# A ReLU-and-sum kernel rewritten on its own semaphores, with clamp and sum split between two engines in three 64 KB buffers

## Chip, cores, metric

One core of a Trainium2 chip. The metric is the device time of one execution in microseconds (us), lower is better. A profile's "span" runs from the first to the last instruction of the program. The time is a little longer than the span. Times are medians.

## The reference

```python
x = np.random.randn(32, 512, 1024).astype(np.float32)
return np.sum(np.maximum(x, 0), axis=-1)      # (32, 512), float32
```

That is 16,384 rows of 1024 numbers, 67.1 MB to read and 64 KB to write. Each of the 128 partitions gets 128 rows.

## The kernel before

The rows are loaded in blocks: seven of 16 rows (64 KB per partition, 8 MB in all), then 8, 4, 2 and 1 rows, then the last row in four column pieces. Blocks of 16 and 8 rows share two buffers. Each row is handled whole by one engine: even rows by ScalarE (ReLU with an accumulated sum), odd rows by VectorE (max with 0, summed). A framework decides the waits.

```python
io_pool = ctx.enter_context(tc.tile_pool(name="io", bufs=2))
...
        nc.scalar.activation(out=out_ap, in_=in_ap, func=Relu,
                             accum_out=res[:, m : m + 1])           # line 71
...
        nc.vector.tensor_scalar(out=out_ap, in0=in_ap, scalar1=0.0, scalar2=None,
                                op0=max, op1=add, accum_out=accum_out)  # line 79
...
    for j, cpd in enumerate(chunks):             # 16 x7, then 8, 4, 2, 1
        xt = io_pool.tile([P, cpd, D], fp32, tag="io", ...)
        nc.sync.dma_start(out=xt, in_=...)                          # line 95
        for c in range(cpd):
            m = m0 + c
            if m == NT - 2:
                act_op(...)
                nc.scalar.dma_start(out=out2d[:, 0 : NT - 2], ...)  # first store
            elif (c % 2) == 0: act_op(xt[:, c, :], xt[:, c, :], m)
            else:              dve_op(xt[:, c, :], xt[:, c, :], res[:, m : m + 1])
...
    for i in range(np_ - 1):                     # pieces 244, 252, 260 wide
        dve_op(ptiles[i], ptiles[i], last[:, pieces[-1] + i : ...])
    dve_op(last, last, res[:, m_last : m_last + 1])   # 268 + three partial sums
    nc.sync.dma_start(out=out2d[:, NT - 2 : NT], in_=res[:, NT - 2 : NT])
```

The four pieces are summed one after the other: the first three leave a partial sum each beside the fourth, which adds them up. The last store waits for that.

## Time and profile before

| | before |
|---|---|
| time, median (4 runs) | 163.43 us (163.22 to 163.71) |
| span of the profiled run | 161.5 us |
| VectorE / ScalarE busy | 46% / 43% |
| load queue, share of 16 DMA engines | 96.9% |

From the profile's page: the span, the busy line, the busy tenths of DMA in 40 slices, and the queue list (name, packets, MB, share).

```profile
span 161.5 us, 347 instructions
DVE 74.3 (46%) x134; ACT 69.0 (43%) x129; POOL 0.2 (0%) x4
DMA  8997997996997997997996997997997997999990
q1 hardware_dynamic: 2304, 67.11, 96.9%
q14 instruction: 2, 0.02, 0.0%
```

The DMA line dips to 7 now and then only because a slice of 4.0 us counts the 2.42 us packets that start in it, and some slices hold fewer starts. The table of stretches, cut at the landings of the blocks, is plainer (columns: start and end, length, busy time and count of each engine, granted clock, DMA share, GB/s):

```profile
core 0: us, DVE busy (x) ACT busy (x) POOL busy (x), PEclk, DMA share, GB/s
22.20:41.60 19.40, 9.21 (x16) 8.42 (x16) 0.00 (x0) 1.00 1.00 432
...
119.60:138.90 19.30, 9.21 (x16) 8.42 (x16) 0.00 (x0) 1.00 0.98 423
...
157.50:161.50 4.00, 1.57 (x8) 1.15 (x2) 0.00 (x0) 1.00 0.10 22
```

The load stream is full from the first to the last block, and both engines are idle half of the time. The chain of waits that ended last shows the end of it (start, length, what):

```profile
41.61 9.22 DVE xt L79 x16
...
50.88 29.41 DMA xt<-in_x_dram
...
130.74 26.82 DMA p<-in_x_dram
157.56 0.02 issue
157.58 1.14 DVE p L79 x6
158.72 0.02 issue
158.74 0.43 DVE p L79
```

The wait of those sums, from the list of waits (engine, what waited, for what: us in total, times, longest):

```profile
DVE p L79 <- DMA p<-in_x_dram: 0.4, 1, 0.4
```

Lines with "issue" in a chain are moments in which the profile shows nothing that the engine waited for.

Read the chain from the end: the last piece sum (started 158.74) closes 1.6 us of sums, which wait for the landing of the pieces at 157.56. A load is asked for 9.2 us after the landing of the block whose buffer it takes, then takes 29.4 us, because about 10 us of it is queueing behind the block before. The queue is never empty. The groups by form give the price of one row on each engine (mean ns of one after the comma):

```profile
L79 DVE TENSOR_SCALAR_CACHE_REDUCE xt<-xt 128x1024 f32<-128x1024 f32 x63 | 72.6, 1216 | 84.5 <-DMA xt<-in_x_dram 84.2
L71 ACT ACTIVATE xt<-xt 128x1024 f32<-128x1024 f32 x64 | 66.7, 1043 | 89.0 <-DMA xt<-in_x_dram 89.0
```

### The profile page before, as it was taken

What the parts mean: (1) busy time and instruction counts of PE and PEld (TensorE: products, weight loads), DVE (VectorE), ACT (ScalarE), POOL (GpSimd) and SP (SyncE); (2) the same over time, 40 slices, a digit from 0 to 9 for tenths busy, and PEclk for the clock granted to TensorE, in tenths of its full rate; (3) what the DMA queues carried; (4) which work ended last, traced back from release to release, by engine and by line L of the source; (5) the groups of instructions that cost most, each with busy time, mean ns of one, the idle gap of its engine ahead of it and who ended that gap; (6) DMA issues with size and microseconds to landing.
All of it is one profiled execution on the core that took longest, in us unless ns stands there. A gap on an engine that the chain in (4) does not pass through costs nothing.

```text
span 161.5 us, 347 instructions
## 1 busy us (share of the span) xinstructions
DVE 74.3 (46%) x134; ACT 69.0 (43%) x129; POOL 0.2 (0%) x4
## 2 busy tenths in 40 slices
DVE  0000049700695008940099101991039900598983
ACT  3000049500693008920099001990039700596882
POOL 0000000000000000000000000000000000000000
DMA  8997997996997997997996997997997997999990
GB/s 308 471 503 308 487 487 308 503 503 292 503 503 308 487 503 325 471 519 308 471 519 296 487 503 325 471 503 341 454 503 341 454 503 308 430 438 406 406 359 22
DMA packets 2450, 67.19 MB, mean 416 GB/s; under 512 B 528, under 2 KB 1040, under 8 KB 1168
## 3 DMA queue, kind: packets, MB, share of 16 engines
q1 hardware_dynamic: 2304, 67.11, 96.9%
q10 hardware_dynamic: 144, 0.06, 0.1%
q14 instruction: 2, 0.02, 0.0%
HBM read 67.11 MB, written 0.07 MB: 416 GB/s over the span
## 4 chain that ended last, share of the span: by engine, by line
DMA 79%; DVE 18%; SPq 1%; issue 0%; DVEq 0%
DMA xt<-in_x_dram 62%; DVE xt L79 17%; DMA p<-in_x_dram 17%; SPq L95 1%; DVE p L79 1%; DVEq L79 0%; DVEq L16 0%
## 5 line engine op out<-in xcount | busy, mean ns | idle before, releaser
L79 DVE TENSOR_SCALAR_CACHE_REDUCE xt<-xt 128x1024 f32<-128x1024 f32 x63 | 72.6, 1216 | 84.5 <-DMA xt<-in_x_dram 84.2
L71 ACT ACTIVATE xt<-xt 128x1024 f32<-128x1024 f32 x64 | 66.7, 1043 | 89.0 <-DMA xt<-in_x_dram 89.0
L71 ACT ACTIVATION_READ_ACCUMULATOR xt<-xt 128x1 f32 x64 | 11.9, 187 | 0.0
L79 DVE DVE_READ_ACCUMULATOR xt<-xt 128x1 f32 x63 | 5.2, 83 | 0.0
L79 DVE TENSOR_SCALAR_CACHE_REDUCE p<-p 128x244 f32<-128x244 f32 (+3 forms) x4 | 1.6, 420 | 0.4 <-DMA p<-in_x_dram 0.4
L71 ACT ACT_TABLE_LOAD x1 | 1.3, 1283 | 0.8 <-PEq L143 0.8
L79 DVE DVE_READ_ACCUMULATOR p<-p 128x1 f32 x4 | 0.3, 82 | 0.0
L143 POOL MEMSET const-bfloat16-1.0<- 128x1 bf16 x1 | 0.1, 101 | 0.0
L143 POOL MEMSET const-uint8-127<- 128x1 uint8 x1 | 0.1, 101 | 0.0
L143 POOL MEMSET const-float32-0.0<- 128x1 f32 x1 | 0.1, 98 | 0.2 <-issue 0.2
L143 POOL MEMSET const-float32-1.0<- 128x1 f32 x1 | 0.1, 98 | 0.0
## 6 DMA issues: line engine op xcount, KB each, us to landing
xt<-in_x_dram SPq DMA_DIRECT2D x1, 4096.0 KB, 19.6
xt<-in_x_dram SPq DMA_DIRECT2D x1, 2048.0 KB, 24.2
xt<-in_x_dram SPq DMA_DIRECT2D x1, 1024.0 KB, 26.2
xt<-in_x_dram SPq DMA_DIRECT2D x1, 512.0 KB, 27.0
p<-in_x_dram SPq DMA_DIRECT2D x1, 134.0 KB, 10.0
p<-in_x_dram SPq DMA_DIRECT2D x1, 130.0 KB, 26.5
p<-in_x_dram SPq DMA_DIRECT2D x1, 126.0 KB, 26.7
p<-in_x_dram SPq DMA_DIRECT2D x1, 122.0 KB, 26.8
```

The source lines that it names most:

```text
L71: nc.scalar.activation(out=out_ap, in_=in_ap, func=mybir.ActivationFunctionType.Relu, accum_out=res[:, m : m + 1],)
L79: nc.vector.tensor_scalar(out=out_ap, in0=in_ap, scalar1=0.0, scalar2=None, op0=mybir.AluOpType.max, op1=mybir.AluOpType.add, accum_out=ac ...
L95: nc.sync.dma_start(out=xt, in_=xv[:, m0 * D : (m0 + cpd) * D].rearrange("p (c d) -> p c d", c=cpd),)
L143: nc = _bacc.Bacc("TRN2", target_bir_lowering=False, num_devices=1)
```

## The change

The intent as the diff shows it: far fewer instructions and waits. The framework's scheduling is dropped for hand-placed semaphores; there are three 64 KB buffers instead of two; in the first six blocks ScalarE clamps 16 rows (8 rows in the last three blocks) in one instruction and VectorE sums them in one; the seventh block is done by rows, ten on ScalarE and six on VectorE; the tail and the pieces are as before; both stores are issued by SyncE.

```diff
+ROWS = 16
+NBUF = 3
+STEPS = [16, 16, 16, 8, 8, 8]
+ACT_ROWS = 10
+TAIL = [8, 4, 2, 1]
+PIECES = [244, 252, 260, 268]
...
+    for j, step in enumerate(STEPS):
+        buf = bufs[j % NBUF]
+        loaded = load(buf[:, :, :], xv[:, m : m + ROWS, :], j >= NBUF and freed[j - NBUF])
+        for c in range(0, ROWS, step):
+            clamp(buf[:, c : c + step, :], loaded if c == 0 else None)   # ScalarE, line 77
+            total(buf[:, c : c + step, :], m + c, step)   # VectorE tensor_reduce, line 85
+        freed.append(n_dve)
+        m += ROWS
...
+    for c in range(ROWS):                                 # block 6
+        first = loaded if c in (0, ACT_ROWS) else None
+        if c < ACT_ROWS:
+            act_row(buf[:, c, :], m + c, first)           # line 92
+        else:
+            dve_row(buf[:, c, :], res[:, m + c : m + c + 1], first)   # line 102
...
+    nc.sync.wait_ge(sems.act, n_act - 1)
+    nc.sync.dma_start(out=out2d[:, : NT - 2], in_=res[:, : NT - 2]).wait_op(
+        sems.dve, n_dve, "sem-ge"
+    ).then_inc(sems.stored, 16)
...
+    nc.sync.wait_ge(sems.act, n_act)
+    nc.sync.dma_start(out=out2d[:, NT - 2 :], in_=res[:, NT - 2 :]).wait_op(
+        sems.dve, n_dve, "sem-ge"
+    ).then_inc(sems.stored, 16)
+    nc.sync.wait_ge(sems.stored, 32)
...
-    io_pool = ctx.enter_context(tc.tile_pool(name="io", bufs=2))
-            elif (c % 2) == 0:
-                act_op(xt[:, c, :], xt[:, c, :], m)
-            else:
-                dve_op(xt[:, c, :], xt[:, c, :], res[:, m : m + 1])
```

Blocks are numbered 0 to 6 below.

More of the change, by code (lines that the diff above doesn't have):

```diff
@@ L1 @@
-from contextlib import ExitStack
 import concourse.bass as bass
 import concourse.tile as tile
-from concourse import bass_utils, mybir
-from concourse._compat import with_exitstack
+from concourse import mybir
+F32 = mybir.dt.float32
+RELU = mybir.ActivationFunctionType.Relu
+MAX, ADD = mybir.AluOpType.max, mybir.AluOpType.add
+P = 128
+ROWS = 16
[4 more added lines that the diff above has]
+PIECES = [244, 252, 260, 268]
 EARLY = 1
 def kernel(tc: tile.TileContext, x: bass.AP, out: bass.AP):
-    trace_relu_sum(tc, x, out)
+    nc = tc.nc
+    sems = Semaphores(tc)
@@ L15, with __init__ @@
     tc.close()
     tc.compile()
-    issue_ahead_of_the_barrier(tc, EARLY)
+    nc.cur_bb = nc.bb_map[tc.start_bb_name]
+    body = nc.cur_bb.bb.instructions
+    ends = list(body)
+    body.clear()
+    relu_sum(nc, sems, x, out)
+    body.extend(ends)
+    issue_ahead_of_the_barrier(tc, EARLY)
+class Semaphores:
+    def __init__(self, tc: tile.TileContext):
+        n = len(STEPS) + 1 + len(TAIL) + len(PIECES)
+        self.loads = [tc.alloc_semaphore(f"load{i}") for i in range(n)]
+        self.act = tc.alloc_semaphore("act")
+        self.dve = tc.alloc_semaphore("dve")
+        self.stored = tc.alloc_semaphore("stored")
@@ new lines, in relu_sum, with load, clamp, total @@
+def relu_sum(nc, sems: Semaphores, x: bass.AP, out: bass.AP):
+    x_flat = x.flatten_outer_dims()
+    N, D = x_flat.shape
+    NT = N // P
+    assert N == P * NT == P * (ROWS * (len(STEPS) + 1) + sum(TAIL) + 1)
+    assert sum(TAIL) == ROWS - 1 and sum(PIECES) == D
+    xv = x_flat.rearrange("(p m) d -> p m d", p=P)
+    out2d = out.rearrange("b s -> (b s)").rearrange("(p m) -> p m", p=P)
+    bufs = [nc.alloc_sbuf_tensor(f"io{i}", [P, ROWS, D], F32) for i in range(NBUF)]
+    res = nc.alloc_sbuf_tensor("res", [P, NT], F32)
+    extra = len(PIECES) - 1
+    parts = [
+        nc.alloc_sbuf_tensor(f"piece{i}", [P, w + extra * (i == extra)], F32)
+        for i, w in enumerate(PIECES)
+    ]
+    n_load = n_act = n_dve = 0
+    def load(dst, src, after=None):
+        nonlocal n_load
+        dma = nc.sync.dma_start(out=dst, in_=src)
+        if after:
+            dma.wait_op(sems.dve, after, "sem-ge")
+        dma.then_inc(sems.loads[n_load], 16)
+        n_load += 1
+        return sems.loads[n_load - 1]
+    def clamp(ap, loaded):
+        nonlocal n_act
+        i = nc.scalar.activation(out=ap, in_=ap, func=RELU)
+        if loaded is not None:
+            i.wait_op(loaded, 16, "sem-ge")
+        i.then_inc(sems.act, 1)
+        n_act += 1
+    def total(ap, m, n):
+        nonlocal n_dve
+        nc.vector.tensor_reduce(
+            out=res[:, m : m + n], in_=ap, axis=mybir.AxisListType.X, op=ADD
+        ).wait_op(sems.act, n_act, "sem-ge").then_inc(sems.dve, 1)
+        n_dve += 1
+    def act_row(ap, m, loaded):
+        nonlocal n_act
+        i = nc.scalar.activation(
+            out=ap, in_=ap, func=RELU, accum_out=res[:, m : m + 1]
+        )
+        if loaded is not None:
+            i.wait_op(loaded, 16, "sem-ge")
+        i.then_inc(sems.act, 1)
+        n_act += 1
+    def dve_row(ap, accum_out, loaded):
+        nonlocal n_dve
+        i = nc.vector.tensor_scalar(
+            out=ap,
+            in0=ap,
+            scalar1=0.0,
+            scalar2=None,
+            op0=MAX,
+            op1=ADD,
+            accum_out=accum_out,
+        )
+        if loaded is not None:
+            i.wait_op(loaded, 16, "sem-ge")
+        i.then_inc(sems.dve, 1)
+        n_dve += 1
+    freed = []
+    m = 0
+    for j, step in enumerate(STEPS):
[6 more added lines that the diff above has]
+        m += ROWS
+    j = len(STEPS)
+    buf = bufs[j % NBUF]
+    loaded = load(buf[:, :, :], xv[:, m : m + ROWS, :], freed[j - NBUF])
+    for c in range(ROWS):
[4 more added lines that the diff above has]
+            dve_row(buf[:, c, :], res[:, m + c : m + c + 1], first)
+    m += ROWS
+    buf = bufs[(j + 1) % NBUF]
+    c0 = 0
+    for n in TAIL:
+        loaded = load(
+            buf[:, c0 : c0 + n, :],
+            xv[:, m + c0 : m + c0 + n, :],
+            None if c0 else freed[j + 1 - NBUF],
+        )
+        for c in range(c0, c0 + n):
+            first = loaded if c < c0 + 2 else None
+            if c % 2 == 0:
+                act_row(buf[:, c, :], m + c, first)
+            else:
+                dve_row(buf[:, c, :], res[:, m + c : m + c + 1], first)
+        c0 += n
+    col = 0
+    arrived = []
+    for part, w in zip(parts, PIECES):
+        arrived.append(load(part[:, :w], xv[:, NT - 1, col : col + w]))
+        col += w
+    nc.sync.wait_ge(sems.act, n_act - 1)
+    nc.sync.dma_start(out=out2d[:, : NT - 2], in_=res[:, : NT - 2]).wait_op(
+        sems.dve, n_dve, "sem-ge"
+    ).then_inc(sems.stored, 16)
+    last, w = parts[-1], PIECES[-1]
+    for i in range(extra):
+        dve_row(parts[i][:, :], last[:, w + i : w + i + 1], arrived[i])
+    nc.vector.wait_ge(arrived[-1], 16)
+    before_last = n_dve
+    nc.vector.tensor_scalar(
+        out=last[:, :],
+        in0=last[:, :],
+        scalar1=0.0,
+        scalar2=None,
+        op0=MAX,
+        op1=ADD,
+        accum_out=res[:, NT - 1 : NT],
+    ).wait_op(sems.dve, before_last, "sem-ge").then_inc(sems.dve, 1)
+    n_dve += 1
+    nc.sync.wait_ge(sems.act, n_act)
[3 more added lines that the diff above has]
+    nc.sync.wait_ge(sems.stored, 32)
@@ L36, in issue_ahead_of_the_barrier @@
     opening[at:at] = loads
-@with_exitstack
-def trace_relu_sum(
-    ctx: ExitStack,
-    tc: tile.TileContext,
-    x: bass.AP,
-    out: bass.AP,
-):
-    nc = tc.nc
-    fp32 = mybir.dt.float32
-    P = nc.NUM_PARTITIONS
-    x_flat = x.flatten_outer_dims()
-    N, D = x_flat.shape
-    assert N % P == 0
-    NT = N // P
-    xv = x_flat.rearrange("(p m) d -> p (m d)", p=P)
-    out2d = out.rearrange("b s -> (b s)").rearrange("(p m) -> p m", p=P)
-    big = 16
-    tail = [8, 4, 2, 1]
-    pieces = [244, 252, 260, 268]
-    assert sum(pieces) == D
-    nbig, rem = divmod(NT - sum(tail) - 1, big)
-    assert rem == 0
-    chunks = [big] * nbig + tail
-    io_pool = ctx.enter_context(tc.tile_pool(name="io", bufs=2))
-    res_pool = ctx.enter_context(tc.tile_pool(name="res", bufs=1))
-    res = res_pool.tile([P, NT], fp32)
-    def act_op(in_ap, out_ap, m):
-        nc.scalar.activation(
-            out=out_ap,
-            in_=in_ap,
-            func=mybir.ActivationFunctionType.Relu,
-            accum_out=res[:, m : m + 1],
-        )
-    def dve_op(in_ap, out_ap, accum_out):
-        nc.vector.tensor_scalar(
-            out=out_ap,
-            in0=in_ap,
-            scalar1=0.0,
-            scalar2=None,
-            op0=mybir.AluOpType.max,
-            op1=mybir.AluOpType.add,
-            accum_out=accum_out,
-        )
-    m0 = 0
-    for j, cpd in enumerate(chunks):
-        if cpd >= 8:
-            xt = io_pool.tile([P, cpd, D], fp32, tag="io", name=f"xt{j}")
-        else:
-            xt = io_pool.tile([P, cpd, D], fp32, tag=f"t{cpd}", bufs=1, name=f"xt{j}")
-        nc.sync.dma_start(
-            out=xt,
-            in_=xv[:, m0 * D : (m0 + cpd) * D].rearrange("p (c d) -> p c d", c=cpd),
-        )
-        for c in range(cpd):
-            m = m0 + c
-            if m == NT - 2:
-                act_op(xt[:, c, :], xt[:, c, :], m)
-                nc.scalar.dma_start(out=out2d[:, 0 : NT - 2], in_=res[:, 0 : NT - 2])
-            elif (c % 2) == 0:
-                act_op(xt[:, c, :], xt[:, c, :], m)
-            else:
-                dve_op(xt[:, c, :], xt[:, c, :], res[:, m : m + 1])
-        m0 += cpd
-    m_last = m0
-    assert m_last == NT - 1
-    base = m_last * D
-    np_ = len(pieces)
-    wlast = pieces[-1] + (np_ - 1)
-    ptiles = []
-    col = 0
-    for i, w in enumerate(pieces):
-        shape_w = w if i < np_ - 1 else wlast
-        pt = io_pool.tile([P, shape_w], fp32, tag=f"p{i}", bufs=1, name=f"p{i}")
-        ptiles.append(pt)
-        nc.sync.dma_start(out=pt[:, 0:w], in_=xv[:, base + col : base + col + w])
-        col += w
-    last = ptiles[-1]
-    for i in range(np_ - 1):
-        dve_op(ptiles[i], ptiles[i], last[:, pieces[-1] + i : pieces[-1] + i + 1])
-    dve_op(last, last, res[:, m_last : m_last + 1])
-    nc.sync.dma_start(out=out2d[:, NT - 2 : NT], in_=res[:, NT - 2 : NT])
```

## The prediction

> **What bounds the kernel now.** The load stream. The table of stretches shows, between the landings of the 8 MB blocks (22.2, 41.6, 61.0, 80.4, 100.2, 119.6, 138.9 us), a DMA share of 0.98 to 1.00 and 423 to 432 GB/s, while in each 19.4 us VectorE is busy 9.2 us and ScalarE 8.4 us. In the trace's packet records a 64 KB packet takes 2.42 us and the next follows without a gap from 1.0 us to 157.5 us. Each load is asked for as soon as VectorE frees a buffer (the chain of waits: 9.22 us of VectorE after a landing), 10 us before the stream would run dry. So an earlier request gains nothing. After the stream come only four piece sums (157.58 to 159.18), a store (issue to landing 1.4 us) and the closing: span 161.5.
>
> **What the change does.** For six blocks, one ScalarE pass clamps 16 (later 8) rows, and VectorE then sums them: serial per block, and each engine touches every element.
> - ScalarE: 1024 columns take 1043 ns now. The Trainium skill, "ScalarE: Activation LUTs", section "What ACT_TABLE_LOAD costs", gives 186 ns + 0.833 ns per column, which fits; estimate 13.8 us for 16 rows, 7.0 for 8.
> - VectorE: the piece sums (407 ns at 244 columns, 435 at 271) give 1.04 ns per column. "VectorE: DVE Perf Modes", section "The perf-mode tier table", has tensor_reduce at one element per cycle only; estimate 17.15 us for 16 rows, 8.6 for 8, back to back. No run shows this instruction yet.
>
> So VectorE goes from 9.2 to 17.2 us per 19.4 us block: it nearly becomes a second limit.
>
> **Critical path, worked through with today's landings.** A block of 16-row steps is free about 31 us after it lands; with three buffers the stream has about 38.8 us. Block 2 ends on VectorE at 61.0+13.9+17.2 = 92; blocks 3 to 5 queue behind it without a gap: 109, 126.5, 144. All are 6 to 11 us before their loads are needed, so I expect no stream gap. But VectorE reaches block 6 (landed 138.9) only at 144: its six rows end at about 150.7, the tail of 8 at 155.2, the tail of 4 at 157.5, of 2 at 158.6, the pieces at 160.2, against 159.18 now. ScalarE's ten rows end at 149.3 and it has caught up by 155.6. Loss about 1 us.
>
> **Gains.** Few instructions: the two 8 KB instruction fetches at 86.3 and 86.7 us (the queue list's "instruction: 2"), which put 0.3 to 0.6 us on two load packets, should disappear; the last-finishing engine could then end the last piece some 0.4 us sooner, but VectorE's backlog would hide this. The hand-written end may save 0.1 to 0.2 us. Moving the first store to SyncE is neutral: it is issued just ahead of the last.
>
> **Prediction: 164.2 us (about +0.5%), 8 in 10 between 162.8 and 165.8.** Faster by over 2%: 0.01; within 2%: 0.95; slower by over 2%: 0.04.
>
> **What would show it.** Right: DMA share near 1 to 157 us; the large clamps 13.8 and 7.0 us, the sums about 17.1 and 8.6 us; VectorE idle only in blocks 0 to 2, then without a gap from 75 us to the end; the piece sums waiting for VectorE itself and not for a load; no instruction fetch mid-run. Wrong: VectorE waiting for DMA ahead of the pieces (then the time is about 163); a gap in the stream near 59, 79 or 98 us (then slower).
>
> **What would make it wrong.** The sums a few per cent slower per element: each 1% adds about 0.7 us to the end. Less overhead between sums than I assume, or a shorter end: 163. Contention between the two engines and the stream, which today's constant packet times do not show.

## The result

| | before | after |
|---|---|---|
| time, median (4 runs each) | 163.43 us | 164.20 us (164.01 to 164.24) |
| span of the profiled run | 161.5 us | 162.4 us |
| last piece sum ends | 159.18 us | 159.98 us |
| from there to the end of the span | 2.34 us | 2.40 us |

The ratio is 1.0044, with a 95% interval of 1.0026 to 1.0061: slower by about 0.4%, clear of noise but far within 2%.

The same lines of the page after the change:

```profile
span 162.4 us, 151 instructions
DVE 119.5 (74%) x43; ACT 103.8 (64%) x46; POOL 0.2 (0%) x4
DMA  8998997998998999899899899899799798999970
q1 hardware_dynamic: 2448, 67.18, 96.5%
```

Less than half the instructions, but VectorE went from 74 to 119 us of work. The line for instruction fetches is gone from the queue list (q1 now also holds the first store, which ScalarE's queue had before). The stretches, again cut at the landings:

```profile
41.60:61.00 19.40, 17.30 (x2) 13.86 (x1) 0.00 (x0) 1.00 1.00 432
...
80.40:99.70 19.30, 19.30 (x2) 13.92 (x2) 0.00 (x0) 1.00 1.00 435
99.70:119.10 19.40, 19.40 (x4) 13.99 (x3) 0.00 (x0) 1.00 1.00 432
...
148.20:157.50 9.30, 9.30 (x19) 8.84 (x17) 0.00 (x0) 1.00 0.96 390
157.50:162.40 4.90, 2.44 (x10) 0.47 (x2) 0.00 (x0) 1.00 0.07 16
```

The stream still runs full and its blocks land every 19.4 us. But from 80.4 to 157.5 us VectorE is busy for the whole of every stretch, and it still has 2.44 us to do after 157.5, where it had 1.57. The chain that ended last now passes through VectorE, not through the loads:

```profile
61.01 13.87 ACT io L77
74.88 0.02 issue
74.90 68.78 DVE res L85 x7
143.68 14.55 DVE io L102 x25
158.23 0.18 issue
158.41 0.09 DVE io L102
158.50 1.02 DVE piece L102 x6
159.51 0.02 issue
159.54 0.43 DVE piece L173
```

From 74.90 us to the end VectorE never waits for anything: seven sums without a gap, then 13 rows, then the pieces. The groups by form and the complete list of VectorE's waits:

```profile
L85 DVE TENSOR_REDUCE res<-io 128x16 f32<-128x16384 f32 x3 | 51.7, 17220 | 40.5 <-ACT io L77 40.5
L85 DVE TENSOR_REDUCE res<-io 128x8 f32<-128x8192 f32 x6 | 51.6, 8679 | 0.0
L77 ACT ACTIVATE io<-io 128x8192 f32<-128x8192 f32 x6 | 41.8, 7022 | 16.3 <-DMA io<-in_x_dram 16.3
L77 ACT ACTIVATE io<-io 128x16384 f32<-128x16384 f32 x3 | 41.6, 13856 | 31.2 <-DMA io<-in_x_dram 31.2
DVE res L85 <- ACT io L77: 40.5, 3, 36.2
```

The wait of the piece sums for their load (0.4 us before the change) is not in that list any more. That is the signature of the backlog: the pieces had landed and VectorE came late.

### The profile page after: what moved, and what is told of

Same layout as the page of the kernel before. It is cut to its first block, busy times and chain, and to the rows that moved or that the text cites. A ratio compares the mean times of both kernels' runs of the same rounds, so it can differ in the third digit from the quotient of the medians.

```text
span 162.4 us, 151 instructions
## 1 busy us (share of the span) xinstructions
DVE 119.5 (74%) x43; ACT 103.8 (64%) x46; POOL 0.2 (0%) x4
## 4 chain that ended last, share of the span: by engine, by line
DVE 52%; DMA 25%; ACT 17%; another core or an unknown queue 3%; issue 0%; DVEq 0%
DVE res L85 42%; DMA io<-in_x_dram 25%; ACT io L77 17%; DVE io L102 9%; DVE piece L102 1%; DVE piece L173 0%; DVEq L28 0%
## 5 line engine op out<-in xcount | busy, mean ns | idle before, releaser
L85 DVE TENSOR_REDUCE res<-io 128x8 f32<-128x8192 f32 (+1 forms) x9 | 103.2, 11526 | 40.5 <-ACT io L77 40.5
L77 ACT ACTIVATE io<-io 128x8192 f32<-128x8192 f32 (+1 forms) x9 | 83.4, 9300 | 47.5 <-DMA io<-in_x_dram 47.5
L92 ACT ACTIVATE io<-io 128x1024 f32<-128x1024 f32 x18 | 18.8, 1048 | 5.9 <-DMA io<-in_x_dram 5.9
L102 DVE TENSOR_SCALAR_CACHE_REDUCE io<-io 128x1024 f32<-128x1024 f32 x13 | 14.9, 1220 | 0.0
L92 ACT ACTIVATION_READ_ACCUMULATOR io<-io 128x1 f32 x18 | 3.4, 191 | 0.0
L102 DVE DVE_READ_ACCUMULATOR io<-io 128x1 f32 x13 | 1.2, 89 | 0.0
L102 DVE TENSOR_SCALAR_CACHE_REDUCE piece<-piece 128x244 f32<-128x244 f32 (+2 forms) x3 | 1.1, 416 | 0.0
```

The costliest lines, as they stand in the source:

```text
L77: i = nc.scalar.activation(out=ap, in_=ap, func=RELU)
L85: nc.vector.tensor_reduce(out=res[:, m : m + n], in_=ap, axis=mybir.AxisListType.X, op=ADD).wait_op(sems.act, n_act, "sem-ge").then_inc(se ...
L92: i = nc.scalar.activation(out=ap, in_=ap, func=RELU, accum_out=res[:, m : m + 1])
L102: i = nc.vector.tensor_scalar(out=ap, in0=ap, scalar1=0.0, scalar2=None, op0=MAX, op1=ADD, accum_out=accum_out,)
```

## The experiments

Theory: the end is late because of VectorE's backlog, an unbroken chain from 74.9 us. Rivals: the load stream's end, the first store on SyncE, the closing, or the new skeleton as such.

A warning on how to read them. The time minus the span is a constant of each program, but not the same for all: 1.73 to 1.83 us in every run of before and 1.74 to 1.82 in every run of after, but 1.94 to 2.10 in e1 to e5, 2.11 to 2.15 in e7, 2.21 to 2.50 in e6, and 1.64 to 1.83 in e9 to e12. The programs differ only in row counts or in a few instructions, and neither the cause of the offset nor a link to the question was found. Mechanisms are therefore read from spans and traces; times and ratios, which contain the offset, are given beside them. Before ran beside each group of experiments, at medians of 163.53 (e1 to e4), 163.31 (e5 to e7 and the control) and 163.35 us (e9 to e12).

### The changed kernel again, beside the step sizes (control)

> Control: the changed kernel unaltered, on the same chip as the step-size runs. Every theory: 0.6 to 1.1 us above before (ratio about 1.004 to 1.006), span 162.4 us, no instruction fetch mid-run.

Measured: 164.23 us, ratio 1.0053 (1.0036 to 1.0070), span 162.3. The result repeats.

### e1: one row from VectorE to ScalarE

```diff
-ACT_ROWS = 10
+ACT_ROWS = 11
```

> One row of block 6 moves from VectorE to ScalarE. Backlog theory: each row is 1.14 us of an unbroken VectorE chain, so the last piece sum ends at about 158.84 us instead of 159.98, VectorE still with no wait or almost none ahead of the pieces; time about 1.1 us less than after (163.1, ratio to before about 0.998). Rival, the end is set by the load stream or by the store and the closing: within 0.2 us of after (164.2).

Measured: 163.41 us, ratio 0.9998 (0.9982 to 1.0014), span 161.3: 1.1 us below after's 162.4, as the backlog theory has it. The last piece sum started at 158.46 and so ended at 158.89 (expected 158.84), with no wait for a load ahead of the pieces:

```profile
158.46 0.43 DVE L173 TENSOR_SCALAR_CACHE_REDUCE piece<-piece 128x271 f32<-128x271 f32 x1
```

The time fell by about 0.8 only, since this program's offset is 2.0 instead of 1.8 us. One row's worth of VectorE work is the whole loss and a little more.

### e2: two rows from ScalarE to VectorE

```diff
-ACT_ROWS = 10
+ACT_ROWS = 8
```

> Two rows of block 6 move from ScalarE to VectorE. Backlog theory: 2 x 1.14 us later, last piece sum ends at 162.3, time about 166.5 (ratio to before about 1.018). Rival (stream, store or closing set the end): within 0.3 us of after (164.2).

Measured: 166.87 us, ratio 1.0202 (1.0187 to 1.0216), span 164.8, the last piece sum ending at 162.43 (expected 162.3). The span rose by 2.4 us for two rows of 1.14 (from the start of one row to the start of the next in the trace); about 0.2 us of it is that in this run VectorE's chain began at 75.09 instead of 74.90.

```profile
162.00 0.43 DVE L173 TENSOR_SCALAR_CACHE_REDUCE piece<-piece 128x271 f32<-128x271 f32 x1
```

Every row counts fully, and with one row less (e1) the end came earlier by one row. So nothing else was bounding the end; the rivals, stream, store and closing, are out for this kernel.

### e3: the first store back on ScalarE's queue

```diff
-    nc.sync.wait_ge(sems.act, n_act - 1)
-    nc.sync.dma_start(out=out2d[:, : NT - 2], ...
+    nc.scalar.wait_ge(sems.act, n_act - 1)
+    nc.scalar.dma_start(out=out2d[:, : NT - 2], ...
```

> After with only the first store put back on ScalarE's queue. Backlog theory: the store is not what ended last, within 0.1 us of after (164.2, ratio 1.004). Rival, both stores on one queue delay the end: about 0.3 to 0.8 us faster than after, that is, at the time of before (163.4) or below.

Measured: 164.41 us, ratio 1.0054 (1.0041 to 1.0066), span 162.4, the same as after's. Where the first store is issued is neutral.

### e4: two rows from VectorE to ScalarE

```diff
-ACT_ROWS = 10
+ACT_ROWS = 12
```

> Two rows moved to ScalarE. Backlog theory: VectorE would be free at 156.1 us, before the pieces land (last packet of the first piece at 156.64 in after), so VectorE now waits for the stream there and the gain saturates: last piece sum ends at about 158.75, time about 163.0, no more than 0.2 us better than with 11 rows. A rival in which every row counts fully would give another 1.1 us (162.0).

Measured: 163.91 us, ratio 1.0023 (1.0009 to 1.0036), span 161.7. The main point held: VectorE now waits 0.45 us for the pieces, and the gain saturates. But the time is not 163.0, and the span is worse than with 11 rows. The timeline of the end shows why:

```profile
157.19 0.41 DVE L102 TENSOR_SCALAR_CACHE_REDUCE piece<-piece 128x244 f32<-128x244 f32 x1 [0.45 <-DMA piece<-in_x_dram]
...
158.18 1.04 ACT L92 ACTIVATE io<-io 128x1024 f32<-128x1024 f32 x1
158.35 0.43 DVE L173 TENSOR_SCALAR_CACHE_REDUCE piece<-piece 128x271 f32<-128x271 f32 x1
158.36 0.34 SPq L164 DMA_DIRECT2D out_dram<-res  x1
159.38 0.34 SPq L185 DMA_DIRECT2D out_dram<-res  x1
```

VectorE was done at 158.78, but the last store was issued only at 159.38, when ScalarE had finished its last row. With 12 rows ScalarE is the late one. My expectation had left that engine out.

### e5: smaller steps in the last clamped block only

```diff
-STEPS = [16, 16, 16, 8, 8, 8]
+STEPS = [16, 16, 16, 8, 8, 4]
```

> Only the last clamped block (block 5) in steps of 4 rows instead of 8; the steps of 16 stay. Backlog theory: VectorE's chain has no gap from the end of ScalarE's third 16-row pass (74.9 us) on, so finer steps late can't help; two more instructions at about 0.07 us each: 0.0 to 0.3 us later than the control. Rival, what costs is the serial clamp-then-sum of the last block: about 2 us earlier at block 6, so about 1.1 us faster than the control.

Measured: 164.61 us, ratio 1.0075 (1.0058 to 1.0091), span 162.5. Nothing gained: VectorE's sums run without a gap from 74.94 for 68.90 us (68.78 in after), so they end 0.16 us later.

```profile
74.94 68.90 DVE L85 TENSOR_REDUCE res<-io 128x16 f32<-128x16384 f32 x9 [2.14 <-ACT io L77]
```

A chain that has no gap can't be shortened by letting a part of it start earlier.

### e6: steps of 8 and a last block of 4

```diff
-STEPS = [16, 16, 16, 8, 8, 8]
+STEPS = [8, 8, 8, 8, 8, 4]
```

> Steps of 8 in blocks 0 to 4, of 4 in block 5. Backlog theory: without the 16-row steps VectorE has idle time before each block (block 4 summed by about 124.1 us instead of 126.5), so block 5 ends at about 141.5 instead of 143.7 and the gain saturates at the landing of the pieces: last piece sum at about 158.8, span 161.2, 1.1 to 1.2 us faster than the control, at about before's time. Rival (serial time of the last block alone): the same gain here, so this run counts only together with the one that changes block 5 alone.

Measured: span 161.2, as expected, and 163.83 us, ratio 1.0028 (1.0010 to 1.0046), because this program's offset is 2.2 to 2.5 us. In the timeline VectorE waits about 2 us before each of blocks 1 to 4, reaches block 6 at 141.33 instead of 143.59, and waits for the pieces:

```profile
157.23 0.41 DVE L102 TENSOR_SCALAR_CACHE_REDUCE piece<-piece 128x244 f32<-128x244 f32 x1 [0.43 <-DMA piece<-in_x_dram]
```

The same edit of block 5 that gave nothing in e5 gives the whole 1.1 us of span here, because the 16-row steps ahead of it are gone.

### e7: steps of 8 everywhere

```diff
-STEPS = [16, 16, 16, 8, 8, 8]
+STEPS = [8, 8, 8, 8, 8, 8]
```

> Steps of 8 in all six blocks. Backlog theory with the serial time of block 5 as its other bound: block 5 landed at 119.06, plus 7.0 for the first clamp, plus two sums of 8.65, gives 143.45 instead of 143.68: only 0.2 us faster than the control (span 162.2), although VectorE now idles before every block. Rival, the 16-row steps alone made the backlog: 1.1 us faster.

Measured: span 162.2, 164.40 us, ratio 1.0062 (1.0045 to 1.0079; offset 2.1). VectorE reached block 6 at 143.35 (after: 143.59), as calculated, although it waited about 2.1 us for ScalarE before every block after the first.

```profile
126.15 17.28 DVE L85 TENSOR_REDUCE res<-io 128x8 f32<-128x8192 f32 x2 [2.07 <-ACT io L77]
```

So two bounds lie on top of each other in after: the gapless chain since block 2, and the serial clamp and sum of block 5 (119.1 + 7.0 + two sums). Of the step sizes, a change that removes one bound alone gains 0.2 us or nothing; only both together give the 1.1 us. (A row taken off VectorE after both, as in e1, gives it too.)

### e9: two buffers instead of three

```diff
-NBUF = 3
+NBUF = 2
```

> After with two 64 KB buffers instead of three. A block in 16-row steps is free 31 us after it lands and one in 8-row steps about 24 us, while the other buffer covers only 19.4 us of stream, so the load stream must stop after each block. Estimate from the measured pieces (13.9 + 17.2 us, a load alone about 21 us from request to landing): about 196 us, between 190 and 202, with VectorE and ScalarE waiting for loads. Rival, the third buffer is not needed: 164 to 166 us.

Measured: 200.58 us (one run, state unknown), span 198.8. The stretches show the stream stop:

```profile
41.50:53.30 11.80, 11.74 (x1) 11.73 (x1) 0.00 (x0) 1.00 0.00 0
```

No byte moves for 11.8 us, until block 0 is summed. My estimate was 4.6 us low. The stream stopped three times, after every second block and not after each as I had expected, and in the chain of waits a load after a stop took 22.25 us from request to landing, not 21. The first packets after each stop took about 3.0 us instead of 2.42. The third buffer is what the split costs in memory: a block is held for 31 us instead of 9.

### e10: the old work in the new skeleton

Every block by rows, alternating, with three buffers, hand-placed semaphores and both stores on SyncE. Only the core of the edit is shown:

```diff
-        for c in range(0, ROWS, step):
-            clamp(buf[:, c : c + step, :], loaded if c == 0 else None)
-            total(buf[:, c : c + step, :], m + c, step)
+        for c in range(ROWS):
+            first = loaded if c < 2 else None
+            if c % 2 == 0:
+                act_row(buf[:, c, :], m + c, first)
+            else:
+                dve_row(buf[:, c, :], res[:, m + c : m + c + 1], first)
```

(with `ACT_ROWS = 8`, and each load waiting for both engines.)

> The new skeleton (own semaphores, three buffers, both stores on SyncE) with the old work: every row of every block done whole by one engine, alternating. Backlog theory: no backlog, last piece sum ends at 159.2 as before, span 161.5, ratio to before 0.998 to 1.003; the many instructions bring the two mid-run 8 KB instruction fetches back and with them a last piece that lands about 0.3 to 0.4 us later than in after. Rival, the skeleton itself costs the 0.8 us: ratio 1.004 to 1.006.

Measured: 163.34 us, ratio 1.0002 (0.9989 to 1.0014), span 161.6, the last piece sum ending at 159.15.

```profile
158.72 0.43 DVE piece L181
```

The skeleton, the third buffer and the place of the stores together cost nothing and gain nothing that this interval would show. All of the difference between before and after lies in splitting clamp from sum.

### e11: mid-run instruction fetches put back

A filler: 101 tiny VectorE and 80 tiny ScalarE instructions before block 0, with the steps of e6. They compute nothing that is used.

```diff
+    nc.vector.memset(fill[:, :], 0.0).then_inc(sems.fill, 1)
+    for i in range(100):
+        nc.vector.memset(fill_v[:, i : i + 1], 0.0)
+    nc.scalar.wait_ge(sems.fill, 1)
+    for i in range(80):
+        nc.scalar.activation(out=fill_act[:, i : i + 1], in_=fill[:, i : i + 1], func=RELU)
```

> Steps of 8 and 4 as in the stream-limited run, plus 101 tiny VectorE and 80 tiny ScalarE instructions in the first 20 us, while both wait for block 0. They do no useful work; they only make the programs longer, so that instructions have to be fetched mid-run. If the fetches are what makes before's last piece land 0.4 us later than after's (last packet 158.13 against 157.72): mid-run fetches appear, a load packet beside each is stretched by 0.3 to 0.6 us, and the last packet ends at 158.0 to 158.3 instead of 157.80, the last piece sum 0.1 to 0.5 us later. If not: the last packet stays at 157.7 to 157.9.

Measured: 163.23 us, ratio 0.9990 (0.9977 to 1.0003), span 161.4. Two fetches appeared, at 6.7 and 9.2 us, and the load packet that started 0.3 us after each took 2.95 and 2.66 us instead of 2.42. The last packet ended at 157.98 us and the last piece sum at 159.04, 0.2 us later than in e6: at the lower edge of what I expected. The run does not settle it, because packets slow down elsewhere too: in e12 the last packet ended at 158.25 with no fetch before the stream's end, after a group of load packets of 2.7 to 3.1 us at 40 us. In the other three-buffer runs without a mid-run fetch it ended between 157.72 and 157.97. In all six mid-run fetches of before, e10 and this run, the packet that began as the fetch ended took 0.24 to 0.60 us longer than 2.42.

The packet records of before's trace go further than that. Put the ends of its 64 KB packets in order and take them in rounds of sixteen, one for each DMA engine (the trace does not name the engine of a packet). From 14.65 to 87.16 us the last of each round ends 0.06 to 0.07 us after the last but one. The second fetch ended at 86.96; the packet that began then took 3.02 us and ended at 89.98, 0.40 us after the last but one. From there on the last of each round is 0.38 to 0.44 us behind, to the end of the 64 KB packets at 138.36. In the last piece, eight packets in a row end at 157.81 to 158.12, when all others have ended by 157.67. So in this trace the 0.4 us is the lag of the packet beside the fetch, never made up. In e12 the lag left by the slow group at 40 us (0.32 us) is kept to the end in the same way, without a fetch.

### e12: one block less in the split

```diff
-STEPS = [16, 16, 16, 8, 8, 8]
+STEPS = [16, 16, 16, 8, 8]
...
+    for j, act_rows in ((5, ACT_ROWS), (6, 8)):    # blocks 5 and 6 by rows
```

> The split of clamp and sum taken back in one block only, block 5, which is done by rows (10 on ScalarE, 6 on VectorE) as block 6 is; block 6 then 8 and 8. Backlog theory: VectorE is through block 4 at 126.5 us and through block 5's six rows at about 133.4, so it waits at block 6 and again ahead of the pieces: last piece sum at about 158.8, span 161.2, that is 1.1 to 1.2 us below after and 0.2 to 0.3 below before. Rival, the skeleton or the clamp-sum blocks before it cost the time: span stays at 162.3.

Measured: 163.23 us, ratio 0.9984 (0.9970 to 0.9997), spans of the five timed runs 161.2 to 161.8. The backlog is gone: VectorE waits 5.1 us at block 6 and, as before the change, for the pieces.

```profile
138.95 1.22 DVE L102 TENSOR_SCALAR_CACHE_REDUCE io<-io 128x1024 f32<-128x1024 f32 x1 [5.09 <-DMA io<-in_x_dram]
...
157.69 0.41 DVE L102 TENSOR_SCALAR_CACHE_REDUCE piece<-piece 128x244 f32<-128x244 f32 x1 [0.41 <-DMA piece<-in_x_dram]
```

The profiled run, the slowest of the five, ended its last piece sum at 159.28, later than the 158.8 I expected, because the piece landed later. Of these runs it is the one whose interval lies below before's time: 0.16% below before and 0.6% below after (0.9984 / 1.0044). But part of this is its offset, 1.64 to 1.73 us against 1.73 to 1.82 in before beside it: the mean spans are 161.5 and 161.6, so a gain over before is not shown. The stream bounds it as it bounds before.

## Why the prediction was right

The prediction was 164.2 us, and 164.20 was measured. Point by point:

- **The load stream is the bound and an earlier request gains nothing.** Held. After: share near 1 and landings every 19.4 us, as before. The old work with three buffers (e10) is at ratio 1.0002.
- **The price of the new instructions.** Held. The clamp of 16 rows was put at 13.8 us from the Trainium skill, "ScalarE: Activation LUTs", section "What ACT_TABLE_LOAD costs"; the trace has 13.856, and 7.022 for 8 rows. The sum was put at 17.15 and 8.6 us back to back, from the slope of the piece sums and from "VectorE: DVE Perf Modes", section "The perf-mode tier table (the rule you actually need)", which has tensor_reduce at its basic rate only. The trace has 17.220 and 8.679 us as durations; back to back, (68.78 - 17.22) / 6 = 8.59.
- **The backlog.** Held at each station, predicted against measured: VectorE reaches block 6 at 144 / 143.6; its six rows done at 150.7 / 150.4; tail of 8 at 155.2 / 155.0; of 4 at 157.5 / 157.3; of 2 at 158.6 / 158.4; pieces at 160.2 / 160.0. The loss at the last piece sum was put at about 1 us and was 0.80. e1 and e2 show that the end moves with VectorE's load, row by row.
- **No gap in the stream with three buffers.** Held; e9 shows the gap that two buffers give.
- **The first store is neutral.** Held (e3).
- **The hand-written end saves 0.1 to 0.2 us.** Wrong in size: it saved nothing, 2.40 us from the last piece sum to the end of the span against 2.34. That and the backlog being 0.2 us smaller than predicted cancel, so that the total fits better than its terms is luck.
- **The instruction fetches disappear.** Held. The last packet of the last piece ended at 157.72 instead of 158.13, and VectorE's lateness hid it. Before's packet records show this 0.4 us as the lag of the packet beside a fetch (under e11); slow packets without a fetch can leave such a lag too (e12).

What the prediction did not see: two bounds coincide at block 5 (e5 and e7). A change of step sizes that addresses only one of them gains 0.2 us at most.

## What to carry to other kernels

Where the loads fill all of the time, as here, there is nothing to gain from other work on the engines, and there is something to lose: splitting one pass into two cut the instructions from 347 to 151, but made every element pass both engines, and VectorE's idle half became a backlog that ended after the last load. With one block less in the split (e12) nothing was lost. When an engine goes from half to nearly fully busy, follow it block by block to the end: a chain that never waits pushes each added microsecond into the tail. Before trying a remedy, ask what else would end at the same time, and compare spans too when effects are below half a per cent.

## What the Trainium skill lacked or had wrong

- "VectorE: DVE Perf Modes" gives a rate class for tensor_reduce and a general cycle table, but no time measured for it. Here, float32 in SBUF: 17.220 us for 16 sums of 1024, 8.679 for 8 of 1024, so 1.04 ns per element and about 0.15 us once per instruction; 8.59 us back to back.
- "ScalarE: Activation LUTs" has 186 ns + 0.833 ns per column: the page names no largest size for which this was measured. Here it holds at 16,384 columns (13.856 us measured, 13.834 by its formula).
- "DMA: Bandwidth & Descriptors", section "Specifications", has 512 B as the least transfer for the full rate. Here packets of 976 B took 45 ns (21.7 GB/s per engine) and packets of 64 KB 2.42 us (27.1 GB/s), so nearly twice that size is still at 80%.
- The same page's section "Queues, rings and completion order" names row 14 as the runtime's, with refills. Neither it nor any other page was found to say what a fetch costs the loads beside it. Here a mid-run fetch of 8 KB took 0.31 us, and the load packet just after it 0.24 to 0.60 us longer than its 2.42.
- No page was found to explain the offset between span and time: 1.8 us in before and after, 2.0 to 2.5 in near-copies of after.
